# Filter generation at the start: the two table subtractions, the first weights' sums and two fetches change engine and place

## The chip, the cores and the metric

One NeuronCore of a Trainium2 chip runs the whole program. The metric is the device time of one execution in microseconds, lower is better; the median of a few executions stands for a kernel.

## What is computed

Four trunk layers follow each other over 512 latent and 256 context tokens of width 1024: latent attention, windowed attention, a gated long convolution, and latent attention again. Each has an adaLN modulation from `w_mod`. Only the long convolution's filters matter here. They depend on weights and positions alone, so the kernel makes them at its very start:

```python
z = jnp.concatenate([t, jnp.cos(bands * w), -jnp.sin(bands * w)], axis=-1)
h = jnp.sin(freq * (z @ f_w1 + f_b1))
h = jnp.sin(freq * (h @ f_w2 + f_b2))
h = (h @ f_w3).astype(jnp.float32).reshape(n, 2, C_ORDER, C_WIDTH)
return h * jnp.exp(-t[:, :, None, None] * deltas)
...
k = jnp.concatenate([lag0, h_fwd[1:], jnp.zeros((1, C_WIDTH)), h_bwd[:0:-1]], axis=0)
kf = jnp.fft.rfft(k, axis=0)
```

`n` is 512 for the latent and 256 for the context tokens, and both are done together as 768 columns.

## The kernel before

A Python program writes instructions in priority order; a planner then fixes the order of each engine at compile time, by a simulated timeline: an engine takes the earliest written instruction that is ready in that simulation. On the chip each engine works its list in that order, and waits at the head of it where an operand is late. All loads and stores are issued by SyncE, whose queue is in order too.

Exact fp32 products are made from pairs of a rounded "high" part and the "low" remainder: ScalarE copies a tile to fp32r (high), and VectorE or GpSimd subtracts it from the original (low). Then TensorE does three products (high·high, high·low, low·high).

Staging memory is one arena cut into slots of 1024 words; a slot's next user waits for its last reader.

The start, in the order written in `run`: `conditions` (L362), the first part of `filters` (up to the first `yield`, L1422), `setup` (L370: identity, modulation biases, `g_pre`), and then `M.pump` (L1681), which starts the first two `w_mod` fetches. After that a loop takes one step of the filters, and at given steps a unit of modulation or the first normalisation of a token tile (`pre`).

The first part of `filters`:

- the position network: step 0 is a matmul (L1329), a chain of six VectorE instructions that reduce the argument of the sine (L1333 to L1338), and the sine on ScalarE (L1339); step 1 is the same with the second weights (L1331). After step 1, L1344 and L1345 make the high and low parts of `h2`, the network's output;
- written between the two steps: `load_w3(0, 0)` fetches four blocks of `f_w3` (L1296), GpSimd makes their sum and difference (L1299, L1300), ScalarE and VectorE split it (L1302, L1303); and `load_ft(0)` fetches the first Fourier table (L1313: 128x1024 and 128x256), split by ScalarE (L1314) and GpSimd (L1315);
- after step 1: `load_ft(1)`, the second table, in the same way, and six loads of the decay (L1359).

Then eight groups (`taps`, `spectrum`) follow. `taps` of a group makes six tiles: two matmuls of `h2` with the split weights (L1380), the multiplication with the decay on VectorE (L1382; in two tiles of half the groups also the bias, L1384), the high part on ScalarE (L1386) and the low part on GpSimd for five tiles, on VectorE for one (L1388). Three buffers hold the products. `spectrum` multiplies these with a Fourier table (L1408), the first table for even groups, the second for odd ones, and VectorE and a store finish it (L1412 to L1418). `load_w3` comes again three times, at the odd groups, for the next weights.

The low parts of `h2` (L1345) must be there before the first L1380. The second and third decay tile lie in the memory that the network's tiles `zt`, `h` and `tm` leave.

Of the kernel before, what the change touches and what calls it, by code (L numbers as in the profile page):

```python
# [12 lines left out]
F32 = mybir.dt.float32  # L13
# [3 lines left out]
ALU = mybir.AluOpType  # L17
# [118 lines left out]
class Ring:  # L136
# [6 lines left out]
    def next(self):  # L143
        self.i += 1
        return self.blocks[self.i % len(self.blocks)]
# [125 lines left out]
class Kern:  # L271
# [989 lines left out]
    def filters(self, j):  # L1261

        nc, io = self.nc, self.io
# [15 lines left out]
        h2 = self.rl(T)  # L1279
        ft = self.rl(2 * 2 * 1280)  # L1280
        ftv = ft.v(2, 2, 1280)
# [6 lines left out]

        def load_w3(c, o):

            st = self.fs(1024)
            sv = st.v(2, 512)
            for d in range(2):
                c0 = d * 2048 + o * 1024 + 512 * c
                for half in range(2):
                    nc.sync.dma_start(out=sv[64 * half:64 * half + 64, d], in_=w3[:, c0:c0 + 512])  # L1296
            sd = self.fs(1024)
            sdv = sd.v(2, 512)
            nc.gpsimd.tensor_tensor(sdv[:, 0], sv[:, 0], sv[:, 1], op=ALU.add)  # L1299
            nc.gpsimd.tensor_tensor(sdv[:, 1], sv[:, 0], sv[:, 1], op=ALU.subtract)  # L1300
            wv = w3r.next().v(2, 2, 512)
            nc.scalar.activation(wv[:, 0], sdv, AF.Copy)  # L1302
            nc.vector.tensor_tensor(wv[:, 1], sdv, wv[:, 0].bitcast(F32), op=ALU.subtract)  # L1303
            st.free()
            sd.free()
            wvs[c, o] = wv
            biases[c, o] = bias = biasr.next()
            nc.sync.dma_start(out=bias.ap[0:1], in_=io["c_filt_bias"][j, o:o + 1, 512 * c:512 * c + 512])

        def load_ft(i):  # L1310
            for c0, n in ((0, 1024), (1024, 256)):
                st = self.fs(n)
                nc.sync.dma_start(out=st.ap, in_=io["ftab"][:, i, c0:c0 + n])  # L1313
                nc.scalar.activation(ftv[:, i, 0, c0:c0 + n], st.ap, AF.Copy)  # L1314
                nc.gpsimd.tensor_tensor(ftv[:, i, 1, c0:c0 + n], st.ap, ftv[:, i, 0, c0:c0 + n].bitcast(F32), op=ALU.subtract)  # L1315
                st.free()

        two_pi = 2 * math.pi
# [5 lines left out]
        for step in range(2):  # L1324
            for c0, n in CH:
                ps = self.a()[:, 0:n]
                for i, r in enumerate((lower, upper)):
                    if step == 0:
                        nc.tensor.matmul(ps[r], w1, zt.ap[:, TH * i + c0:TH * i + c0 + n], start=True, stop=True, skip_group_check=True)  # L1329
                    else:  # L1330
                        nc.tensor.matmul(ps[r], w2[r], h.ap[r, c0:c0 + n], start=True, stop=True, skip_group_check=True)  # L1331
                hv, tv = h.ap[:, c0:c0 + n], tm.ap[:, c0:c0 + n]
                nc.vector.tensor_scalar(hv, ps, fv[:, 2 * step:2 * step + 1], freq, op0=ALU.add, op1=ALU.mult)  # L1333
                nc.vector.tensor_scalar(tv, hv, 1.0 / two_pi, magic, op0=ALU.mult, op1=ALU.add)
                nc.vector.tensor_scalar(tv, tv, magic, None, op0=ALU.subtract)
                nc.vector.scalar_tensor_tensor(hv, tv, -c1, hv, op0=ALU.mult, op1=ALU.add)
                nc.vector.scalar_tensor_tensor(hv, tv, -c2, hv, op0=ALU.mult, op1=ALU.add)
                nc.vector.tensor_scalar(hv, hv, 3.1415925, -3.1415925, op0=ALU.min, op1=ALU.max)  # L1338
                nc.scalar.activation(hv, hv, AF.Sin)  # L1339
                if step == 1:  # L1340

                    for i, (r, o) in enumerate(((lower, upper), (upper, lower))):
                        c = slice(TH * i + c0, TH * i + c0 + n)
                        nc.scalar.activation(h2.ap[r, c], hv[r], AF.Copy)  # L1344
                        nc.vector.tensor_tensor(h2.ap[o, c], hv[r], h2.ap[r, c].bitcast(F32), op=ALU.subtract)  # L1345
            if step == 0:
                load_w3(0, 0)
                load_ft(0)
        for b in (zt, h, tm):
            b.free()  # L1350
        load_ft(1)
        LTS = [4, 5, 0, 1, 2, 3]
        decr = [self.fl(512) for _ in range(8)]
        tmps = Ring(self, "fl", 512, 3)
# [12 lines left out]
        def taps(c, o, e):  # L1367
# [3 lines left out]
            if e == 1 and (c, o) != (1, 1):  # L1371
                load_w3(*((c, 1) if o == 0 else (1, 0)))
                if (c, o) == (0, 1):
                    load_dec(1, 0)
                    load_dec(1, 1)
# [285 lines left out]
    def run(self, layers=(0, 1, 2, 3)):  # L1661
        nc, io = self.nc, self.io
        n = len(layers)
        self.layers = layers
        self.xd = {layers[0]: [io["xc"][P * t:P * t + P] for t in range(6)]}
        for i, L in enumerate(layers):
            if i < n - 1:
                d = self.dram.tile([T, D], F32, name=f"x{L + 1}")
                self.xd[L + 1] = [d[P * t:P * t + P] for t in range(6)]
            else:  # L1670
                self.xd[L + 1] = [io["out"][P * t:P * t + P] for t in range(io["out"].shape[0] // P)]
        L = layers[0]
        self.plan_mod(layers)
        self.set_swing("R")
        h = self.h_alloc()
        self.conditions()
        steps = self.filters(0) if 2 in layers else iter(())
        next(steps, None)
        self.setup()
        self.M.cap_d = self.M.look_d = 2  # L1680
        self.M.pump()  # L1681
        for i, L in enumerate(layers):
            kind, j = L % 3, L // 3
            ctx_out = L < DEPTH - 1
            if kind == 0:
                self.want_A(L, j, ctx_out)
            elif kind == 1:
                self.want_B(L, j)
            else:
                self.want_C(L, j)  # L1690
        L = layers[0]

        def pres():
            ts = [0, 1, 2, 3, 4, 5]
            self.W.cap_d = 2
            xts = [self.load_x(L, t) for t in ts[:1]]
            yield
            for i, t in enumerate(ts):
                if i < 5:
                    xts.append(self.load_x(L, ts[i + 1]))  # L1700
                self.pre(L, t, xts[i], h)
                xts[i].free()
                if i == WP:
                    self.turns_f = 1
                    self.W.pump()
                    self.turns_f = 6
                yield

        start = iter(pres())
        for i in range(99):  # L1710
            if i == LS:
                self.setup_late()
            if i == MI[3] - 1:
                self.M.cap_d = self.M.look_d = 0
            if i in MI:
                for _ in self.mod_ab_unit(L, MI.index(i)):
                    pass
            if i >= PS and (i - PS) % PD == 0:
                next(start, None)
            if i in WX:  # L1720
                self.W.cap_d, self.W.cap_w = WX[i]
                self.W.pump(*WX[i])
            if next(steps, 1) == 1 and i > PS + 13:
                break
        self.M.cap_d = self.M.look_d = 1
        for i, L in enumerate(layers):
            kind, j = L % 3, L // 3
            last = i == n - 1
            ctx_out = L < DEPTH - 1
            if kind == 0:  # L1730
                h = self.layer_A(L, j, h, ctx_out, last)
            elif kind == 1:
                h = self.layer_B(L, j, h, last)
            else:
                h = self.layer_C(L, j, h, last)
# [103 lines left out]
```

## Time and profile before

| | us |
|---|---|
| median of 3 runs | 1951.43 (1951.01 to 1953.01) |
| the profiled execution | 1952.31 |
| its span | 1950.4 |

The profile is one execution: its span starts with the first instruction of an engine, and some 1.9 us of the time lie around it. A row of the timeline says when an instruction began, how long it (or the run of equal ones, "x4") took, on which engine and line, what it wrote and read, and in brackets how long the engine had been idle and what released it. Engines are PE (TensorE), PEld (its weight loads), DVE (VectorE), ACT (ScalarE), POOL (GpSimd); SPq is SyncE's queue of transfers.

### The profile page before, as it was taken

Reading aid. Unit: us, or ns where it says so; the run is one execution under the profiler, and the core shown is the slowest. Engines: PE = TensorE matmul, PEld = TensorE weight load, DVE = VectorE, ACT = ScalarE, POOL = GpSimd, SP = SyncE. Lnnn points to the kernel's source line nnn. Section 1 sums busy time; section 2 is a strip of 40 time slices with the busy share of each in tenths; the row PEclk is TensorE's granted clock in tenths of the full one; section 3 lists DMA queues with packets and bytes.
Section 4 is the critical chain, followed back from the end, with each engine's and each line's share of the span. In section 5 each row is a group of like instructions: output and inputs, shape, how many; then the busy total and the mean of one; then the engine's idle time right before and its main releaser. Section 6 shows DMA issues by size and latency. Waiting matters only on the chain. (4 is left out here: it accounts for less than half of the span.)

```text
span 1950.4 us, 30304 instructions
## 1 busy us (share of the span) xinstructions
PE 1818.6 (93%) x11628; PEld 1576.9 (81%) x11628; DVE 1169.7 (60%) x2365; ACT 814.3 (42%) x1688; POOL 519.7 (27%) x523
## 2 busy tenths in 40 slices
PE   5879799999999899999989999999989899999998
PEld 3657588999988888888868789999988677889986
DVE  6694134777755277777665456655566553477663
ACT  3473132555544255665654522222222352354451
POOL 5561000000213321222231444444434221000120
PEclk9899999999999999999999999999999899999999
DMA  7867431010133122222363622222222334310121
GB/s 219 261 172 230 150 80 30 23 33 34 55 108 109 55 65 67 77 77 66 107 207 108 200 81 77 76 76 71 72 64 71 107 127 140 97 33 23 44 66 65
DMA packets 186356, 186.31 MB, mean 96 GB/s; under 512 B 16600, under 2 KB 164952, under 8 KB 186212
## 3 DMA queue, kind: packets, MB, share of 16 engines
q1 hardware_dynamic: 186212, 184.39, 30.6%
q8 instruction: 91, 1.49, 0.3%
q14 instruction: 53, 0.43, 0.1%
HBM read 160.24 MB, written 24.12 MB: 95 GB/s over the span
## 5 line engine op out<-in xcount | busy, mean ns | idle before, releaser
L588 PE MATMUL pb<-arena_r 128*128 128x512 f32 (+1 forms) x1488 | 280.9, 342 | 1.9 <-DVE arena_f L567 1.0
L341 ACT ACTIVATE arena_r<-pa 128x384 fp32r<-128x384 f32 (+2 forms) x382 | 175.5, 479 | 206.1 <-PE pa L909 67.9
L588 PEld LDWEIGHTS pb<-arena_r 128*128 128x128 f32 x1488 | 230.1, 190 | 32.9 <-ACT arena_r L1462 1.5
L342 DVE TENSOR_TENSOR arena_r<-pa,arena_r 128x384 fp32r<-128x384 f32 (+2 forms) x382 | 199.5, 536 | 81.7 <-ACT arena_r L341 79.8
L588 PE MATMUL pa<-arena_r,swing_R 128*128 128x512 f32 (+1 forms) x816 | 165.9, 355 | 0.6 <-DVE arena_r L342 0.4
L588 PEld LDWEIGHTS pa<-arena_r,swing_R 128*128 128x128 f32 x816 | 132.2, 188 | 21.8 <-DVE arena_r L342 0.6
L884 PE MATMUL pb<-arena_r 128*128 128x384 f32 (+1 forms) x720 | 141.5, 337 | 3.0 <-ACT arena_r L341 1.8
L606 PE MATMUL pb<-arena_r 128*128 128x512 f32 x552 | 133.7, 394 | 1.6 <-ACT arena_r L230 1.3
L233 POOL TENSOR_TENSOR swing_R<-arena_f,swing_R 128x1024 fp32r<-128x1024 f32 (+1 forms) x33 | 76.2, 2313 | 192.0 <-ACT swing_R L230 142.5
L884 PEld LDWEIGHTS pb<-arena_r 128*128 128x128 f32 x720 | 119.1, 188 | 5.1 <-ACT arena_r L341 2.5
L606 PEld LDWEIGHTS pb<-arena_r 128*128 128x128 f32 x552 | 102.5, 188 | 25.1 <-ACT arena_r L230 1.8
L679 POOL TENSOR_TENSOR arena_f<-arena_f 128x128 f32<-128x128 f32 (+1 forms) x44 | 20.9, 475 | 362.8 <-DVE small L892 178.6
L233 POOL TENSOR_TENSOR arena_r<-swing_F,arena_r 128x1024 fp32r<-128x1024 f32 x36 | 88.0, 2448 | 88.7 <-ACT arena_r L230 83.5
L358 POOL TENSOR_SCALAR small<-small 128x1 f32<-128x1 f32 x68 | 17.8, 261 | 348.0 <-ACT trash L564 139.5
L923 PE MATMUL pa<-arena_r 128*128 128x256 f32 x624 | 91.5, 286 | 2.1 <-DVE arena_r L342 2.1
L923 PEld LDWEIGHTS pa<-arena_r 128*128 128x128 f32 x624 | 81.9, 189 | 4.8 <-ACT arena_r L341 2.5
L1079 PE MATMUL pa<-swing_R,arena_r 128*128 128x256 f32 x576 | 80.3, 289 | 5.0 <-DVE arena_f L348 3.8
L230 ACT ACTIVATE arena_r<-swing_F 128x1024 fp32r<-128x1024 f32 x39 | 41.4, 1063 | 103.9 <-PE pb L588 63.3
L888 DVE TENSOR_REDUCE small<-pb 128x1 f32<-128x768 f32 (+1 forms) x80 | 67.5, 845 | 21.6 <-PE pb L884 20.7
L891 ACT ACTIVATE arena_f<-pb,small 128x768 f32<-128x768 f32 (+1 forms) x80 | 65.2, 817 | 33.1 <-DVE small L889 26.7
L1079 PEld LDWEIGHTS pa<-swing_R,arena_r 128*128 128x128 f32 x576 | 72.9, 192 | 7.3 <-DVE arena_f L348 5.2
L442 PE MATMUL pa<-arena_f,cst 128*32 128x256 f32 x744 | 56.7, 405 | 21.7 <-DMA arena_f<-in_w_mod_dram 21.6
(268 smaller groups left out, 4210.0 us busy)
## 6 DMA issues: line engine op xcount, KB each, us to landing
arena_f<-in_w_mod_dram SPq DMA_DIRECT2D x93, 512.0 KB, 4.7
swing_F<-in_c_w_in_dram SPq DMA_DIRECT2D x31, 512.0 KB, 5.0
kd<-arena_f SPq DMA_DIRECT2D x48, 256.0 KB, 3.5
arena_f<-in_a_w_in_dram SPq DMA_DIRECT2D x24, 512.0 KB, 3.7
arena_f<-kd SPq DMA_DIRECT2D x16, 768.0 KB, 5.2
arena_f<-in_b_w_in_dram SPq DMA_DIRECT2D x20, 512.0 KB, 3.7
x<-arena_f SPq DMA_DIRECT2D x18, 512.0 KB, 4.2
arena_f<-in_a_w_out_dram SPq DMA_DIRECT2D x16, 512.0 KB
```

The costliest lines, as they stand in the source:

```text
L230: nc.scalar.activation(hi, view, AF.Copy)
L233: eng.tensor_tensor(lo, view, hi.bitcast(F32), op=ALU.subtract)
L341: self.nc.scalar.activation(hi, src, AF.Copy)
L342: self.nc.vector.tensor_tensor(lo, src, hi.bitcast(F32), op=ALU.subtract)
L442: nc.tensor.matmul(ps[32 * j:32 * j + 32, n0:n0 + 256], self.cst[:, 4 * kh + j, :], w[:, j, :], start=(kh == 0), stop=(kh == 1), skip_grou ...
L588: nc.tensor.matmul(out, l, rhs(part, k, i), start=(k == 0 and q == 0), stop=(k == kt - 1 and q == 2))
L606: nc.tensor.matmul(ys[:, 512 * hf:512 * hf + 512], ov[:, a, k - ks.start], wt[:, 0, 512 * hf:512 * hf + 512], start=(k == 0 and q == 0), s ...
L884: nc.tensor.matmul(S[:, 512 * b:512 * b + w], l, r[:, k0 + w * b:k0 + w * b + w], start=(q == 0), stop=(q == 4))
L888: nc.vector.tensor_reduce(mx, Sv, axis=AX.XY, op=ALU.max)
L891: nc.scalar.activation(pr.v(nb, w), Sv, AF.Exp, bias=mx, scale=sc, accum_out=sm)
L923: nc.tensor.matmul(o[:, 0:256], vv[:, a_, kt % 3, P * hh:P * hh + P], ptv[i // nh][:, b_, i % nh], start=(i == 0 and q == 0), stop=(i == n ...
L1079: nc.tensor.matmul(ps[:, 0:256], self.h_at(h, part, k, P * t, P), w, start=(k == 0 and i == 0), stop=(k == KD - 1 and i == 2))
```

## The change

The first weights' sum and difference move from GpSimd to VectorE, and their split is written after step 1 instead of before it. The first table is still fetched between the steps, but its split is written after step 1, with the subtraction on VectorE. The second table's fetch gets a one-column VectorE copy from `h2` into its staging slot, so that the transfer can't start before the first high part of `h2` is there; its subtraction stays on GpSimd. The later three `load_w3` are as before. `M.pump` comes before `setup`.

```diff
         def load_w3(c, o):
 
+            split_w3(c, o, sum_w3(nc.gpsimd, fetch_w3(c, o)))
+
+        def fetch_w3(c, o):
             st = self.fs(1024)
             sv = st.v(2, 512)
             for d in range(2):
                 c0 = d * 2048 + o * 1024 + 512 * c
                 for half in range(2):
                     nc.sync.dma_start(out=sv[64 * half:64 * half + 64, d], in_=w3[:, c0:c0 + 512])
+            return st
+
+        def sum_w3(eng, st):
+            sv = st.v(2, 512)
             sd = self.fs(1024)
             sdv = sd.v(2, 512)
-            nc.gpsimd.tensor_tensor(sdv[:, 0], sv[:, 0], sv[:, 1], op=ALU.add)
-            nc.gpsimd.tensor_tensor(sdv[:, 1], sv[:, 0], sv[:, 1], op=ALU.subtract)
+            eng.tensor_tensor(sdv[:, 0], sv[:, 0], sv[:, 1], op=ALU.add)
+            eng.tensor_tensor(sdv[:, 1], sv[:, 0], sv[:, 1], op=ALU.subtract)
+            st.free()
+            return sd
+
+        def split_w3(c, o, sd):
+            sdv = sd.v(2, 512)
             wv = w3r.next().v(2, 2, 512)
             nc.scalar.activation(wv[:, 0], sdv, AF.Copy)
             nc.vector.tensor_tensor(wv[:, 1], sdv, wv[:, 0].bitcast(F32), op=ALU.subtract)
-            st.free()
             sd.free()
...
-        def load_ft(i):
+        def fetch_ft(i, late):
+            out = []
             for c0, n in ((0, 1024), (1024, 256)):
                 st = self.fs(n)
+                if late:
+
+                    nc.vector.tensor_copy(st.ap[0:64, 0:1], h2.ap[0:64, 0:1].bitcast(F32))
                 nc.sync.dma_start(out=st.ap, in_=io["ftab"][:, i, c0:c0 + n])
+                out.append((i, c0, n, st))
+            return out
+
+        def split_ft(eng, parts):
+            for i, c0, n, st in parts:
                 nc.scalar.activation(ftv[:, i, 0, c0:c0 + n], st.ap, AF.Copy)
-                nc.gpsimd.tensor_tensor(ftv[:, i, 1, c0:c0 + n], st.ap, ftv[:, i, 0, c0:c0 + n].bitcast(F32), op=ALU.subtract)
+                eng.tensor_tensor(ftv[:, i, 1, c0:c0 + n], st.ap, ftv[:, i, 0, c0:c0 + n].bitcast(F32), op=ALU.subtract)
                 st.free()
...
             if step == 0:
-                load_w3(0, 0)
-                load_ft(0)
+                sd0 = sum_w3(nc.vector, fetch_w3(0, 0))
+                ft0 = fetch_ft(0, False)
+        split_w3(0, 0, sd0)
+        split_ft(nc.vector, ft0)
         for b in (zt, h, tm):
             b.free()
-        load_ft(1)
+        split_ft(nc.gpsimd, fetch_ft(1, True))
...
         next(steps, None)
-        self.setup()
         self.M.cap_d = self.M.look_d = 2
         self.M.pump()
+        self.setup()
```

## Rows read from the trace of the kernel before

**Rows 1.** Stretches: length, busy time per engine (instructions), TensorE's clock, DMA share, GB/s.
```profile
10.00:20.00 10.00, 1.38 (x4) 0.13 (x4) 8.37 (x6) 3.67 (x5) 9.72 (x6) 1.00 1.07 368
20.00:60.00 40.00, 34.12 (x180) 23.64 (x181) 30.28 (x49) 18.58 (x32) 24.43 (x19) 1.00 0.69 211
...
240.00:1950.00 1710.00, 1632.33 (x10574) 1444.43 (x10573) 1031.11 (x2130) 715.61 (x1503) 420.12 (x419) 0.99 0.26 80
```

**Rows 2.** Timeline of VectorE, 5 to 26 us: both network steps, first tap.
```profile
6.19 0.68 DVE L1333 TENSOR_SCALAR arena_f<-pa,arena_f 128x384 f32<-128x384 f32 x1 [4.37 <-PE pa L1329]
...
7.29 0.36 DVE L1335 TENSOR_SCALAR arena_f<-arena_f 128x384 f32<-128x384 f32 x1
...
8.87 0.36 DVE L1338 TENSOR_SCALAR arena_f<-arena_f 128x384 f32<-128x384 f32 x1
11.53 0.68 DVE L1333 TENSOR_SCALAR arena_f<-pa,arena_f 128x384 f32<-128x384 f32 x1 [2.30 <-PE pa L1331]
...
13.02 2.40 DVE L1335 TENSOR_SCALAR arena_f<-arena_f 128x384 f32<-128x384 f32 x1
...
16.34 3.35 DVE L1303 TENSOR_TENSOR arena_r<-arena_f,arena_r 128x1024 fp32r<-128x1024 f32 x1
...
20.72 0.36 DVE L1338 TENSOR_SCALAR arena_f<-arena_f 128x384 f32<-128x384 f32 x1
22.29 1.14 DVE L1345 TENSOR_TENSOR arena_r<-arena_f,arena_r 64x384 fp32r<-64x384 f32 x2 [1.20 <-ACT arena_r L1344]
25.86 0.69 DVE L1382 TENSOR_TENSOR arena_f<-pa,arena_f 128x512 f32<-128x512 f32 x1 [2.43 <-PE pa L1380]
```

**Rows 3.** Timeline of GpSimd, 8 to 62 us; then stretches of GpSimd alone (busy, clock, DMA share, GB/s).
```profile
10.28 1.26 POOL L1299 TENSOR_TENSOR arena_f<-arena_f 128x512 f32<-128x512 f32 x1 [8.73 <-DMA arena_f<-in_c_f_w_dram]
...
12.72 7.55 POOL L1315 TENSOR_TENSOR arena_r<-arena_f,arena_r 128x1024 fp32r<-128x1024 f32 x4
28.01 2.52 POOL L1388 TENSOR_TENSOR swing_R<-arena_f,swing_R 128x512 fp32r<-128x512 f32 x2 [7.73 <-ACT swing_R L1386]
...
31.72 2.35 POOL L1300 TENSOR_TENSOR arena_f<-arena_f 128x512 f32<-128x512 f32 x1
...
28.00:45.00 17.00, 16.00 (x11) 1.00 0.69 222
45.00:145.00 100.00, 60.80 (x48) 0.95 0.74 216
```

**Rows 4.** Timeline of VectorE after 30 us; two short stretches, columns as in rows 1.
```profile
30.64 1.69 DVE L1384 SCALAR_TENSOR_TENSOR arena_f<-arena_f 1x512 f32<-1x512 f32 x1
32.25 0.67 DVE L1388 TENSOR_TENSOR swing_R<-arena_f,swing_R 128x512 fp32r<-128x512 f32 x1
...
35.86 1.78 DVE L1303 TENSOR_TENSOR arena_r<-arena_f,arena_r 128x1024 fp32r<-128x1024 f32 x1
...
69.84 1.22 DVE L1303 TENSOR_TENSOR arena_r<-arena_f,arena_r 128x1024 fp32r<-128x1024 f32 x1
...
34.00:36.00 2.00, 1.84 (x24) 0.99 (x16) 2.00 (x5) 1.74 (x3) 2.00 (x3) 1.00 0.09 20
...
69.80:71.10 1.30, 1.14 (x17) 0.56 (x18) 1.30 (x3) 1.04 (x2) 0.71 (x2) 1.00 1.07 321
```

**Rows 5.** Timeline of ScalarE, 11 to 13 us.
```profile
11.56 1.06 ACT L1314 ACTIVATE arena_r<-arena_f 128x1024 fp32r<-128x1024 f32 x1 [1.77 <-DMA arena_f<-in_ftab_dram]
```

**Rows 6.** Timeline of SyncE's queue, 0 to 60 us.
```profile
9.55 1.82 SPq L1359 DMA_DIRECT2D arena_f<-in_decay_dram x4
...
13.59 0.93 SPq L211 DMA_DIRECT2D arena_f<-in_w_mod_dram x2
...
23.49 0.81 SPq L1359 DMA_DIRECT2D arena_f<-in_decay_dram x2
```

**Rows 7.** Transfers issued from 7.6 to 40 us: count, KB each, median us to landing.
```profile
arena_f<-in_decay_dram SPq DMA_DIRECT2D x8, 256.0 KB, 5.8
arena_f<-in_ftab_dram SPq DMA_DIRECT2D x2, 512.0 KB, 5.0
```

## Prediction, made before the changed kernel had been run

> **What bounds the kernel now.** I read the stretches first [rows 1]. From 240 us to the end TensorE is busy 1632.3 of 1710 us, so that part is TensorE's own work, and time saved or lost before it moves it as a block. At the start it is otherwise: between 10 and 20 us TensorE has four matmuls (1.4 us), while GpSimd is busy 9.7 of 10 us, VectorE 8.4, and the DMA engines all the time; from 20 to 60 us TensorE is at 34 of 40 us and the DMA share falls to 0.69. The question is therefore what keeps TensorE from its first tap, and how much of a gain there lives until 240 us.
>
> The timeline of VectorE answers the first half [rows 2]. The first tap needs both parts of h2, and the network's second step makes them. Its six instructions take 3.04 us in step 0 (6.19 to 8.87 + 0.36) and 9.55 us in step 1 (11.53 to 20.72 + 0.36), the same six with L1303 among them. L1335 takes 2.40 us there against 0.36 in step 0; L1303 takes 3.35. All this lies beside GpSimd's four table subtractions, 12.72 to 20.27 [rows 3]. h2 is complete at 22.29 + 1.14 = 23.43.
>
> Is it GpSimd or the full DMA engines that slow VectorE? L1303 tells them apart [rows 4]: 1.78 us at 35.86, with GpSimd busy throughout and a DMA share of 0.09; 1.22 us at 69.84, with a DMA share of 1.07 and GpSimd busy for 0.71 of 1.30 us. So it is GpSimd, and the premise of the change holds.
>
> The Trainium skill (SBUF — State Buffer, Who interferes with whom) has it as a lock: a VectorE instruction with two SBUF inputs, or in a two-port mode, excludes a GpSimd instruction that reads SBUF, and the second to start is blocked fully. The rows of step 1 agree (L1335 waits 2 us, it isn't shared out). The same rule speaks against the change's other end: the second table's subtraction, still on GpSimd, would lie beside L1384, which has two SBUF inputs. It took 1.69 us at 30.64 beside L1300's 2.35, against the 0.67 of VectorE's other 512-column subtraction at 32.25 [rows 4], so by the rule the sum would be 1.0 us worse; without it nothing is lost there.
>
> **The change part by part.**
>
> *Sums on VectorE.* They leave GpSimd (1.26 us each) and cost VectorE what a 128x512 subtraction costs, 0.67 [rows 3, 4]. The weights land by 10.28, so they run from there to 11.62, in the hole before L1333 (11.53): 0.1 us on the path. If that hole were gone they would cost 1.34.
>
> *Step 1 with GpSimd quiet.* From 11.62 the six take step 0's 3.04, to 14.7. Sine, high part and low part follow: from the end of L1338 (21.08) to 23.43 is 2.35 us [rows 2]. That gives h2 at 17.05.
>
> *Three subtractions that VectorE now has beside it.* L1303 (1.22) and the first table (1280 columns, by L1303's rate 1.5) are 2.7 us. They are written behind step 1, but the planner puts ready work into holes. The idle of 1.20 us before L1345 [rows 2] takes one of them. If the rest stands behind L1345, h2 stays at 17.05; if all stand before it, h2 comes at 17.05 + 1.5 = 18.55. I take the middle, 17.8, since nothing in the trace decides it: 5.6 us earlier than 23.43 (bounds 4.9 and 6.4).
>
> *Second table fetched late.* It leaves GpSimd's stretch before the taps and comes back inside them. Its 640 KB start after the first high part of h2, about 16 us, and land about 5 us later by the first table's 5.0 [rows 7], at 21 to 22. ScalarE's copy costs 1.06 [rows 5], so GpSimd gets it at 22 to 23, just when the first L1388 comes due (28.01 − 5.6 = 22.4). What it costs GpSimd has two bounds: by L1299's rate 1280/512 x 1.26 = 3.2 us, by half of 7.55 us 3.8 [rows 3]. From 28 to 45 us GpSimd is busy 16.0 of 17 us, so it has no room for 3.2 to 3.8 there. But in that stretch are the next weights' sums (1.29 and 2.35), which no tap needs until the third group, and after 45 us GpSimd is busy only 61 of 100 us. Where the table stands in the place of these sums and pushes them back, the price is near zero; where it stands ahead of the taps' low parts as well, 3.8. Only the odd groups' spectrum reads the table, and by the order written it comes behind the first taps of the third group. I take 1.4, nearer to zero, because the third group and the slack after 45 us can absorb it.
>
> *The two tiny copies* on VectorE: one column each; bounds are zero and 0.36, what 384 columns take in step 0. They fall into VectorE's 2.43 us hole before the first tap [rows 2]; behind them wait only the transfers. I take zero, 0.7 if the hole is gone.
>
> *Queue of transfers.* Ahead of the taps the queue has 640 KB less, which at 368 GB/s [rows 1] is 1.7 us; the first four decays (issued from 9.55) come earlier, which nobody waits for. Two decays wait for h2's last reader (23.49) [rows 6]. They now start about 5.6 us earlier, but into a queue that is still full, beside the late table. Each 256 KB is 0.7 us at that rate; the second tap needs one of them, behind the first tap, which itself came 2.43 us after h2 [rows 2]. Bounds: zero (the queue has drained) and 1.7 (the table ahead of them); I take zero, since what stands ahead of them was issued 4 us and more before (13.59 and earlier), and keep 1.7 for the range.
>
> *w_mod ahead of setup.* The two fetches at 13.59 go a little earlier, and bmod, gpre and the identity's place in the list later. The first user of w_mod and of bmod is the modulation unit that `run` calls four steps into the filters, which is after h2 in either kernel; nothing waits, zero. Were they to pass the decays they would cost their 1 MB, 2.8 us.
>
> **Sum:** 5.6 − 1.4 = 4.2 us. The profiled execution, 1952.3, becomes 1948.1; against the median, 1951.43 − 4.2 = 1947.2. After 240 us there is nothing to absorb it; between 60 and 240 us the waits for w_mod follow from earlier events and not from a fixed moment, so I let them move along.
>
> **Rivals.** Less than about 0.2% (3.9 us) can't be told from no change.
>
> *A, forecast:* 1945.5 to 1949, chance 0.40, of which 0.24 lies beyond 3.9 us.
>
> *B, the second table takes the place of the first:* GpSimd pays 3.8 us within the taps and the late decays another 0 to 1.7. That leaves 0 to 2 us, about 1950.2. For it: 16 of 17 us busy. Against it: the sums can give way. 0.25.
>
> *C, slower:* engines work in order, and the planner knows only simulated landings. If it puts the second table's copy and subtraction ahead of the first L1386 and L1388, GpSimd stands until the table has landed, then needs 1.06 + 3.2 before the first low part. Before, that came at 28.01. So a landing at 23.7 uses up the whole gain, and each us later costs one; at 28 the time is 1955.7. For it: DMA engines at 1.07. Against it: that landing would be 12 us after the issue, twice the 5.8 seen. A late table read by a spectrum that was planned early acts in the same way. 0.15.
>
> *D, it doesn't do what it says:* VectorE stays slow although GpSimd is quiet, because of the DMA engines. Then the chain keeps its 9.5 us, VectorE has 1.5 us more, and the time is 1953. L1303's two rows speak against it. 0.05.
>
> *E, more:* h2 at 17.05, no price on GpSimd: 6.4 us, 1945. It needs every subtraction in a hole. 0.15.
>
> **How the numbers follow.** Faster by over 0.2%: 0.24 of A, 0.15 of E, 0.03 of B, together 0.42. Within: 0.16 of A, 0.22 of B, 0.04 of D, 0.42. Slower: 0.15 of C and 0.01 of D, 0.16. The likeliest case is A, 1947.2. The range takes in A, B, D, E and the near part of C, where the table lands up to 2.5 us past the point of 23.7: 1943 to 1954. By itself A has 1945.5 to 1949.
>
> **What would show it.** Right: step 1's L1335 at 0.36 us; L1303 at 1.2; h2 complete at 17 to 18.6 us instead of 23.43; the first L1388 at 22 to 23; no GpSimd wait for the table's transfer; TensorE's last waits before 240 us some 4 us earlier. B shows as GpSimd's L1388 of the second group no earlier than before; C as an idle time on GpSimd or ScalarE released by in_ftab; D as L1335 still above 1 us. The forecast is wrong, too, if the planner, starting from other moments, orders the units of modulation or the stores of the filters in another way; the trace of before can't price that, and the range covers it only in part.

## The result: slower by 0.7%, and the profile after

| | before | after |
|---|---|---|
| median, us (4 executions each) | 1951.22 (1946.31 to 1953.01) | 1962.24 (1960.28 to 1964.89) |
| profiled execution | 1952.31 | 1963.88 |
| its span | 1950.4 | 1961.8 |

The ratio of after to before is 1.0071 [1.0057, 1.0086] (95% interval in brackets, here and below). The forecast was 4.2 us faster; it came 11 us slower, and outside the range (1943 to 1954).

Line numbers after the change: L1306, L1307 the weights' sums; L1314, L1315 their split; L1327 the one-column copies, L1328 the fetch of a table, L1334, L1335 its split; L1353 to L1359 chain and sine; L1364, L1365 the parts of `h2`; L1381 the decay; L1402 the tap's matmuls, L1404 times decay, L1406 bias, L1408 high part, L1410 low part; L1430 to L1440 the spectrum.

The timeline of VectorE, which answers [rows 2]:

```profile
10.46 0.69 DVE L1306 TENSOR_TENSOR arena_f<-arena_f 128x512 f32<-128x512 f32 x1 [1.07 <-DMA arena_f<-in_c_f_w_dram]
...
11.68 0.68 DVE L1353 TENSOR_SCALAR arena_f<-pa,arena_f 128x384 f32<-128x384 f32 x1
12.87 1.22 DVE L1315 TENSOR_TENSOR arena_r<-arena_f,arena_r 128x1024 fp32r<-128x1024 f32 x1 [0.51 <-ACT arena_r L1314]
14.01 0.35 DVE L1354 TENSOR_SCALAR arena_f<-arena_f 128x384 f32<-128x384 f32 x1
14.28 1.55 DVE L1335 TENSOR_TENSOR arena_r<-arena_f,arena_r 128x1024 fp32r<-128x1024 f32 x2
15.75 0.35 DVE L1355 TENSOR_SCALAR arena_f<-arena_f 128x384 f32<-128x384 f32 x1
...
19.47 0.21 DVE L1327 COPY arena_f<-arena_r 64x1 f32<-64x1 f32 x2
19.71 0.55 DVE L1365 TENSOR_TENSOR arena_r<-arena_f,arena_r 64x384 fp32r<-64x384 f32 x1
22.70 0.56 DVE L401 CAST maskb<-arena_f 128x768 bf16<-128x768 f32 x1 [2.44 <-DMA arena_f<-in_mask_dram]
23.18 0.68 DVE L1404 TENSOR_TENSOR arena_f<-pa,arena_f 128x512 f32<-128x512 f32 x1
23.89 0.68 DVE L1406 SCALAR_TENSOR_TENSOR arena_f<-arena_f 1x512 f32<-1x512 f32 x1
28.15 1.42 DVE L1404 TENSOR_TENSOR arena_f<-pa,arena_f 128x512 f32<-128x512 f32 x2 [3.58 <-DMA arena_f<-in_decay_dram]
29.60 1.23 DVE L1406 SCALAR_TENSOR_TENSOR arena_f<-arena_f 1x512 f32<-1x512 f32 x1
```

What the change was built for happened: the six instructions of step 1 take 0.35 to 0.68 us each again, and `h2` is complete at 19.71 + 0.55 = 20.26 instead of 23.43. Then three transfers are late. VectorE stands 2.44 us for the mask, which the plan has put ahead of the first tap, and 3.58 us for a decay tile ahead of the second. The mask costs the first tap less than its wait: VectorE begins with the third of TensorE's products, and TensorE has it at 22.42 (the sixth of the eight matmuls in the first line below), so the tap at 23.18 comes 0.8 us late. ScalarE and GpSimd stand for the second table; the timelines (TensorE 18 to 33 us, ScalarE 18 to 32, GpSimd 5 to 36, where before's was [rows 3]):

```profile
19.50 3.78 PE L1402 MATMUL pa<-arena_r 128*128 128x512 f32 x8 [7.96 <-DVE arena_r L1365]
...
26.78 1.36 ACT L1334 ACTIVATE arena_r<-arena_f 128x1024 fp32r<-128x1024 f32 x2 [7.38 <-DMA arena_f<-in_ftab_dram]
28.05 0.61 ACT L1408 ACTIVATE swing_R<-arena_f 128x512 fp32r<-128x512 f32 x1
...
27.92 3.51 POOL L1335 TENSOR_TENSOR arena_r<-arena_f,arena_r 128x1024 fp32r<-128x1024 f32 x2 [26.37 <-ACT arena_r L1334]
31.39 1.27 POOL L1410 TENSOR_TENSOR swing_R<-arena_f,swing_R 128x512 fp32r<-128x512 f32 x1
```

ScalarE was free from 19.40, and the first product lay ready at 24.57 (L1406), but its work list has the table's copy ahead of the first high part. The first tap is still early, 23.18 instead of 25.86, but the first low part on GpSimd starts at 31.39, where before had 28.01. SyncE's queue shows where the transfers stood, and answers [rows 6] (start, time to issue, line, what, how many):

```profile
18.59 0.38 SPq L400 DMA_DIRECT2D arena_f<-in_mask_dram  x1
19.07 1.75 SPq L1299 DMA_DIRECT2D arena_f<-in_c_f_w_dram  x3
20.91 1.01 SPq L1328 DMA_DIRECT2D arena_f<-in_ftab_dram  x2
22.02 0.84 SPq L1381 DMA_DIRECT2D arena_f<-in_decay_dram  x2
```

The table is issued at 20.91, behind the mask and three blocks of the next weights, and the two decays behind the table. The DMA engines are full from 24 us on, while the table and the decays land. Stretches of after (length; busy time and instructions of PE, PEld, DVE, ACT, POOL; TensorE's clock; DMA share; GB/s); those from 10, 20 and 240 us answer to [rows 1]:

```profile
24.00:26.00 2.00, 1.14 (x2) 0.42 (x2) 0.57 (x1) 0.00 (x0) 0.00 (x0) 1.00 1.00 362
26.00:28.00 2.00, 0.00 (x0) 0.00 (x0) 0.00 (x0) 1.22 (x2) 0.08 (x1) 1.00 1.01 319
...
10.00:20.00 10.00, 2.04 (x5) 0.78 (x6) 7.66 (x15) 3.87 (x6) 0.00 (x0) 1.00 0.94 308
20.00:60.00 40.00, 33.30 (x144) 20.76 (x143) 24.13 (x35) 13.73 (x22) 22.44 (x16) 1.00 0.65 194
88.40:161.40 73.00, 59.65 (x277) 42.16 (x278) 55.40 (x91) 42.97 (x80) 40.73 (x35) 0.88 0.66 190
240.00:1961.00 1721.00, 1641.74 (x10652) 1449.89 (x10650) 1035.57 (x2132) 717.41 (x1509) 420.06 (x422) 0.99 0.26 79
```

GpSimd is quiet from 10 to 20 us (0.00 against 9.72 us), and from 240 us on TensorE is busy 95% of the time, as before. In between the loss grows. The table of moments (us from the start; "spectrum" is L1434, L1412 before; "layer" the first normalised tile of the second, third and fourth layer) shows where:

| profiled kernel | `h2` | first low part | first spectrum | 12th | 24th, last | layer 2 | layer 3 | layer 4 | end |
|---|---|---|---|---|---|---|---|---|---|
| before | 23.4 | 28.0 | 32.9 | 83.1 | 149.8 | 559.8 | 1031.4 | 1540.9 | 1950.4 |
| after | 20.3 | 31.4 | 38.7 | 88.4 | 161.4 | 574.4 | 1043.3 | 1552.5 | 1961.8 |

In these two profiles 5.8 us are lost by the first spectrum, another 6.3 us between the 12th and the last and 3.0 in the first layer, and later layers give 3 back. A profile is one execution. Two kernels of the experiments, e11 and e4, run TensorE's list in before's order, and so are two more samples of it: their spans are 1943.7 and 1941.9, the first spectrum comes at 33.4 and 33.7, and the 12th to the last take 65.5 and 65.2 us. The losses of 5.8 and 6.3 us stand clear of that spread; what the later layers give back does not, since layers 2 to 4 took 1590.6 us in before but 1584.9 and 1583.3 in e11 and e4, and 1587.4 in after. The stretch from the 12th to the last spectrum in the kernel before:

```profile
83.10:149.80 66.70, 51.20 (x242) 36.71 (x241) 54.65 (x90) 41.03 (x77) 38.88 (x33) 0.92 0.67 189
```

After does 35 more matmuls in it (e11 and e4, in before's order, 5 and 6 more), so its order is another one, and at a mean clock of 0.88 instead of 0.92.

### The profile page after: what moved, and what is told of

It reads as the page before. It is cut to its first block, busy times and chain, and to the rows that moved or that the text cites. A ratio compares the mean times of both kernels' runs of the same rounds, so it can differ in the third digit from the quotient of the medians.

```text
span 1961.8 us, 30305 instructions
## 1 busy us (share of the span) xinstructions
PE 1829.0 (93%) x11628; PEld 1578.9 (80%) x11628; DVE 1172.5 (60%) x2371; ACT 814.2 (42%) x1688; POOL 508.4 (26%) x519
## 5 line engine op out<-in xcount | busy, mean ns | idle before, releaser
L588 PE MATMUL pa<-arena_r,swing_R 128*128 128x512 f32 (+1 forms) x816 | 165.9, 355 | 0.6 <-DVE arena_r L342 0.4
L606 PE MATMUL pb<-arena_r 128*128 128x512 f32 x552 | 133.7, 394 | 2.1 <-ACT arena_r L230 1.8
L606 PEld LDWEIGHTS pb<-arena_r 128*128 128x128 f32 x552 | 102.5, 188 | 25.4 <-ACT arena_r L230 2.0
L891 ACT ACTIVATE arena_f<-pb,small 128x768 f32<-128x768 f32 (+1 forms) x80 | 65.2, 816 | 33.1 <-DVE small L889 26.7
L1060 PE MATMUL pa<-arena_r,swing_R 128*128 128x512 f32 (+1 forms) x384 | 74.2, 342 | 2.7 <-DVE arena_r L1086 1.1
```

Source lines behind the costliest of these rows:

```text
L588: nc.tensor.matmul(out, l, rhs(part, k, i), start=(k == 0 and q == 0), stop=(k == kt - 1 and q == 2))
L606: nc.tensor.matmul(ys[:, 512 * hf:512 * hf + 512], ov[:, a, k - ks.start], wt[:, 0, 512 * hf:512 * hf + 512], start=(k == 0 and q == 0), s ...
L891: nc.scalar.activation(pr.v(nb, w), Sv, AF.Exp, bias=mx, scale=sc, accum_out=sm)
L1060: nc.tensor.matmul(o, l[:, k], self.h_at(h, part, k, t0, n), start=(k == 0 and i == 0), stop=(k == KD - 1 and i == 2))
```

## The experiments

Two theories. **Late transfers**: the loss is the waits for decay, mask and table at the first taps; remove these and the change gains 0 to 4 us. **Another plan**: the planner starts from other simulated moments and gives the whole program another order, good or bad by some us, whatever happens at the start. All ratios are to the kernel before, run beside on the same chip; its median was 1948.55, 1946.83 and 1947.67 us in the three sets of runs (20, 28 and 25 executions), each on another chip. The traces also give the order in which TensorE ran its 11628 matmuls. The last column counts the places of that list at which a kernel has another matmul than before has (by the text of its source line, its tiles and its shape); after has 541.

| kernel | median, us | ratio | first low part | first spectrum | last | end of profiled span | places |
|---|---|---|---|---|---|---|---|
| e1 table not held | 1955.51 | 1.0035 [1.0020, 1.0050] | 27.4 | 35.3 | 152.1 | 1953.8 | 493 |
| e2 table behind taps | 1960.08 | 1.0056 [1.0032, 1.0080] | 28.5 | 33.6 | 153.0 | 1954.1 | 585 |
| e3 decays moved | 1947.32 | 1.0002 [0.9985, 1.0018] | 22.7 | 39.9 | 151.5 | 1944.0 | 441 |
| e5 both of these | 1978.30 | 1.0166 [1.0123, 1.0210] | 22.7 | 35.3 | 156.6 | 1980.7 | 2010 |
| e14 e3, mask later | 1979.59 | 1.0171 [1.0151, 1.0191] | 25.1 | 35.2 | 152.0 | 1979.9 | 1832 |
| e9 VectorE part only | 1959.64 | 1.0060 [1.0042, 1.0078] | 27.6 | 36.0 | 154.1 | 1950.7 | 493 |
| e13 e9, decays moved | 1952.59 | 1.0025 [1.0012, 1.0039] | 25.5 | 31.7 | 151.3 | 1947.6 | 802 |
| e6 e1, decays moved | 1953.55 | 1.0029 [1.0013, 1.0045] | 25.5 | 31.7 | 152.3 | 1944.8 | 802 |
| e8 hold only | 1949.00 | 1.0012 [0.9997, 1.0027] | 25.8 | 33.3 | 156.1 | 1944.9 | 506 |
| e7 before, decays moved | 1952.70 | 1.0029 [1.0012, 1.0047] | 26.0 | 32.7 | 153.7 | 1943.1 | 580 |
| e11 before, one column | 1948.82 | 1.0007 [0.9994, 1.0020] | 27.7 | 33.4 | 148.6 | 1943.7 | 0 |
| e4 w_mod early only | 1946.74 | 1.0003 [0.9988, 1.0018] | 27.9 | 33.7 | 148.5 | 1941.9 | 0 |

**Is it the late table?** e1 fetches it early again, e2 holds it still longer, behind the first two taps, with the split behind the first group.

```diff
 # e1
-        split_ft(nc.gpsimd, fetch_ft(1, True))
+        split_ft(nc.gpsimd, fetch_ft(1, False))
 # e2, against after
-                    nc.vector.tensor_copy(st.ap[0:64, 0:1], h2.ap[0:64, 0:1].bitcast(F32))
+                    nc.vector.tensor_copy(st.ap[:, 0:1], sds[0, 0, 0][:, 5, 0, 0:1].bitcast(F32))
...
-        split_ft(nc.gpsimd, fetch_ft(1, True))
...
+                if g == (0, 0, 0) and n == 0:
+                    ft1 = fetch_ft(1, True)
                 yield
+            if g == (0, 0, 0):
+                split_ft(nc.gpsimd, ft1)
```

> The changed kernel, but the second table's fetch is not held back (no one-column copies from h2); the table's subtraction stays on GpSimd, written after step 1, and all else is as changed. Theory T (the late table costs it: its transfer goes out at 20.9 us, lands at 26.8, ScalarE and GpSimd stand behind it, and two decays stand behind it in the queue of transfers): ScalarE's 7.4 us wait for in_ftab is gone, the first low part on GpSimd comes at 25 to 28 us instead of 31.4, and the time is 1947 to 1953. Rival P (the planner, started from other moments, orders all later work worse, whatever the table does): the time stays at 1957 or above. Rival V (the subtractions that VectorE took into the network's chain are the cost): h2 at 20 us or later and 1957 or above.

> The changed kernel, but the second table is fetched after the first two taps (its one-column copies read a tap's high part instead of h2) and its split is written behind the first group's taps. T: nothing of the table stands ahead of the first taps' high and low parts, so the first low part comes at 24 to 27 us, and the time is 1945 to 1952; the decays that wait for h2 may still land late, as three blocks of the next weights stand ahead of them. P: 1957 or above. If the decays alone set it (rival D2): the second tap's wait for in_decay stays at 3 us or more and the time is 1952 to 1957.

Half of the loss is gone in e1, and its time lies between the two ranges expected: nothing waits for the table, but `h2` is back at 22.45. The first table on VectorE meets the second one on GpSimd:

```profile
14.04 3.70 DVE L1335 TENSOR_TENSOR arena_r<-arena_f,arena_r 128x1024 fp32r<-128x1024 f32 x2
17.66 0.88 DVE L1355 TENSOR_SCALAR arena_f<-arena_f 128x384 f32<-128x384 f32 x1
...
15.17 2.56 DVE L1335 TENSOR_TENSOR arena_r<-arena_f,arena_r 128x256 fp32r<-128x256 f32 x1
...
15.02 3.29 POOL L1335 TENSOR_TENSOR arena_r<-arena_f,arena_r 128x1024 fp32r<-128x1024 f32 x2 [13.47 <-ACT arena_r L1334]
```

3.70 us where after has 1.55: without the hold the quiet GpSimd isn't had. The 3.70 are two instructions ("x2"). The one of 1024 columns, which began before GpSimd's, took its usual 1.2; the one of 256, which began after it, took 2.56 (third line), where after's took 0.42. In e2 the table is out of the way and the first low part comes 2.9 us earlier than in after, yet the mask (3.27 us) and the decay (1.76 us) still stop VectorE, and another 7.1 us are lost between the last spectrum and the second layer; the time is in the range of the second theory. So the late table explains a part, and what follows it is not simply its shadow.

**Is it the decay behind the table?** The two late decays are the tiles that take over the network's memory. e3 turns the ring of eight blocks by three, so that they lie in memory that nobody uses at that time; e5 does that to e2.

```diff
-            b, lt = decr[(6 * c + n) % 8], LTS[n]
+            b, lt = decr[(6 * c + n + 3) % 8], LTS[n]
...
-                        decr[(6 + 6 + n) % 8].free()
+                        decr[(6 + 6 + n + 3) % 8].free()
```

> The changed kernel, but the decays use their eight blocks from the fourth one on, so that none of the first six has to wait for the memory of the network's tiles; they are all issued early. T: the second tap's 3.6 us wait for in_decay is gone, but ScalarE still waits for the table until 26 us or later, so the first low part stays at 30 us or later and the time falls by no more than 3 us, 1959 to 1963. D2 (the decays set it): 1952 to 1957. P: any time, without relation to these waits.

> Both edits of the two runs before: the second table behind the first taps, and the decays in blocks that nobody else uses. T together with the decays: VectorE waits for no transfer between h2 and the sixth tap, the first low part comes at 23 to 26 us, two to five us before that of the kernel before (28.0), and the time is 1944 to 1949. P: 1957 or above.

e3 is the largest gain among the variants, and only the second theory, which named no time, allows it: all six decays are issued by 11.9 us, none is waited for, the first low part starts at 22.7 and the end is that of the kernel before. Its start is not good, though: the mask (2.79 us), the sinks (3.43 us) and the next weights take the place of the decay, and the first spectrum comes at 39.9, later than in any other. What it gains it gains after that: from the 12th to the last spectrum it takes 60.8 us, before 66.7 and after 73.0, in an order that is neither's (738 places of TensorE's list differ from after's, all but 191 of them ahead of the second layer). So it shows that after's loss can be had back with these two tiles moved, not that their wait alone was the loss. It shows, too, that a first spectrum 7.0 us late need not cost anything at the end.

e5 should have had the best of both and is 1.7% slower, some 30 us. Of these 23 are not at the start. They lie between the second and the third layer, the windowed attention. That stretch in before and in e5 (stretches, columns as above):

```profile
559.80:1031.40 471.60, 443.69 (x3220) 384.90 (x3219) 302.90 (x713) 243.39 (x591) 123.20 (x152) 0.99 0.29 93
...
565.60:1060.30 494.70, 453.48 (x3237) 389.23 (x3236) 305.76 (x714) 244.48 (x593) 123.06 (x152) 0.98 0.28 89
```

TensorE has 17 matmuls more there, is busy 9.8 us longer and stands 41 us instead of 28: no filter, table or decay is touched there. The order is: between these two moments all kernels of the table but e5 and e14, and after too, have before's order of TensorE at every place, and take 466 to 472 us; e5 differs from it at 1071 of 3218 places. That is the second theory, in its plainest form.

**What does another order cost by itself?** e11 changes nothing but one column of zeros written on VectorE; e7 turns the decays in the kernel before; e4 has only `M.pump` ahead of `setup`.

```diff
 # e11
                 load_w3(0, 0)
                 load_ft(0)
+                nc.vector.memset(fv[:, 140:141], 0.0)
 # e4
-        self.setup()
         self.M.cap_d = self.M.look_d = 2
         self.M.pump()
+        self.setup()
```

> The kernel before with one VectorE instruction more, a memset of one column that nobody reads, 0.1 us, behind step 0's chain; everything else is written as before. The planner nevertheless orders most of the program in another way. T: the time stays within 2 us of the kernel before, as no wait is added. P: it moves by 3 us or more, and the move arises after the first taps.

> The kernel before with the decays in their blocks from the fourth one on, as in the run on the changed kernel that gained 13 us by it. T: the second tap of the kernel before doesn't wait for its decay, so there is little to gain: 0 to 3 us under the kernel before. P: any move of 3 us or more, as the plan is another one.

> The kernel before with only w_mod's first fetches ahead of setup. The orders of TensorE, VectorE, ScalarE and GpSimd are those of the kernel before, so both theories give ratio 0.999 to 1.001. The rival price: if w_mod's 1 MB passes the decays or the mask in the queue, the first taps wait up to 2.8 us longer, ratio 1.0015.

The expectation of e11 says that the planner orders most of the program in another way. It did not: in the traces TensorE, ScalarE and GpSimd run before's list at every place, and VectorE's has the one instruction more. So e11 doesn't test another order; it and e4 repeat the kernel before, with no change of time that can be measured. e7 has another order: its first low part comes 2.0 us earlier, its first spectrum 0.2, and its end is 0.29% worse, as the second theory allows and the first does not. From the 12th to the last spectrum it takes as long as after, though no transfer is late in its start (the stretch in e7, columns as above):

```profile
80.80:153.70 72.90, 58.30 (x280) 42.35 (x280) 53.77 (x89) 42.17 (x77) 39.62 (x36) 0.91 0.68 202
```

e4 puts four transfers of SyncE's list in another place and changes no other engine's list, and no time: the early `w_mod` is neutral.

**The parts of the change.** e8 is the hold alone, on the kernel before; e9 the VectorE part alone, with the early table and `setup` first.

```diff
 # e8
                 st = self.fs(n)
+                if i == 1:
+                    nc.vector.tensor_copy(st.ap[0:64, 0:1], h2.ap[0:64, 0:1].bitcast(F32))
 # e9, against after
-        split_ft(nc.gpsimd, fetch_ft(1, True))
+        split_ft(nc.gpsimd, fetch_ft(1, False))
...
+        self.setup()
         self.M.cap_d = self.M.look_d = 2
         self.M.pump()
-        self.setup()
```

> The kernel before with one part of the change alone: the second table's fetch held back by the one-column copies from h2, all else as before. h2 comes at about 21 us, as GpSimd has one table less beside VectorE. T (the late table costs it): ScalarE waits for in_ftab, the first low part comes at 30 us or later instead of 28.0, and the end of the filters (the last of the 24 high parts of the spectrum, 149.8 us before) is 2 to 8 us later; the time is 2 to 8 us above the kernel before. P (the planner's later order sets it): the end of the filters or the later layers move by as much in either direction, without relation to that wait.

> The kernel before with the other part alone: the first sums and the first table's subtraction on VectorE, the second table fetched early and subtracted on GpSimd after step 1, w_mod behind setup as before. h2 at 20 to 22 us, first low part at 26 to 28. T: no loss, the time is 0 to 3 us under the kernel before. P: as in the run without the hold (0.35 per cent above), since the order of the engines is that of another plan: 4 to 10 us above.

The hold alone is the milder part. `h2` is at 21.1, because only half of GpSimd's subtractions lie beside step 1. VectorE waits 1.72 us for a decay, but ScalarE has the first high part ahead of the table's copy, which starts at 25.66 without a wait, and the 4.12 us on GpSimd stand behind the first low part. Its last spectrum is 6.3 us late, yet at the end no loss can be told from the noise (1.0012). The VectorE part alone costs 0.6%, more than either theory expected, although `h2` comes 0.8 us earlier than before. This ratio repeats only roughly: e1 has e9's order on the four engines and differs from it in the same four transfers as e4 from before, and came out at 1.0035 on another chip. The intervals of the two just meet.

**The VectorE part with nothing late.** e13 and e6 are e9 and e1 with the decays turned as in e3. They have the same order on TensorE, VectorE, ScalarE and GpSimd and differ in the place of four transfers in SyncE's list. e14 is e3 with `LS = 12` instead of 2, which writes the mask and the late constants ten steps later.

> VectorE part alone (sums and first table on VectorE, second table fetched early, setup first), with the decay tiles in blocks that the network does not use. Late-transfer theory: what the VectorE part alone loses, 0.6%, is again a wait for a transfer at the first taps, so it goes: ratio to the kernel before 0.999 to 1.001, the first low part on GpSimd at 26 to 27.5 us, the first spectrum by 33. Plan theory: the waits of the start are not it; the loss lies in another order of the whole program, and an edit of the start that changes moments only draws another one: ratio anywhere from 0.998 to 1.01, without regard to when the first spectrum comes.

> The changed kernel with the second table fetched early (no one-column copies) and the decay tiles moved. Late-transfer theory: neither table nor decay can be late; h2 at about 22.5 us, first low part at 26, first spectrum before 33, ratio to the kernel before 0.998 to 1.000. Plan theory: ratio anywhere from 0.998 to 1.01.

> The changed kernel with the decay tiles moved and with the mask and the small late constants (0.8 MB) written ten steps of the filters later. Late-transfer theory: VectorE's wait for the mask and a part of the waits for the next weights and the table go; first low part at 22.7 as with the decays moved alone, first spectrum at 33 to 36 instead of 39.9, ratio to the kernel before 0.997 to 0.999, the first version that is faster. Plan theory: first spectrum earlier, but the end not, ratio 1.000 or above.

e13 and e6 agree with each other, 1.0025 and 1.0029. Neither waits for a decay, mask or table, the first low part is 2.5 us and the first spectrum 1.2 us earlier than before: the start that the prediction wanted, if a smaller one. And both are some 5 us slower at the end than before, run beside them. In the profile of e13 the lead is gone by the 12th spectrum and 1.5 us are lost by the last. So a better start doesn't carry through this kernel by itself, and what undoes it lies behind 32 us. The first theory missed here (0.999 to 1.001 and 0.998 to 1.000); the range of the second, 0.998 to 1.01, holds both, but it is too wide to be much of a test.

e14 has a better start than e3 (first spectrum 35.2, VectorE without a wait for the mask), should have been the first version that is faster, and loses 22.8 us in the windowed attention, like e5. The two have the same order of TensorE there, place by place, and the same length; e3, which has before's order there, for comparison (e14, then e3):

```profile
565.60:1059.90 494.30, 453.76 (x3237) 389.87 (x3236) 306.07 (x713) 244.97 (x593) 122.73 (x152) 0.98 0.28 89
...
559.60:1029.00 469.40, 440.68 (x3219) 382.62 (x3218) 302.66 (x712) 243.07 (x591) 122.75 (x152) 0.99 0.29 94
```

At the end of that layer TensorE's timeline in e14 has a wait of 3.95 us for VectorE's L567, the addition of a finished output tile to its tokens, ahead of the last matmuls (L606):

```profile
1051.97 1.88 PE L494 MATMUL pa<-arena_f,sel 128*128 128x512 f32 x4
1057.80 7.16 PE L606 MATMUL pb<-swing_R,arena_r 128*128 128x512 f32 x18 [3.95 <-DVE arena_f L567]
```

The same wait, 3.95 us, stands in e5 at this layer's end, and in no other kernel. (At the end of the third layer every kernel has one like it, before at 1538.89 with 3.93 us.) That is 4 of the 23 us; the rest is spread over many short waits and the longer busy time. So the 23 us go with this one order of the layer, in both kernels that have it and in none of the others; which places of the order carry them, and why the planner chose it, stays open.

## Why the prediction was wrong

**The reading of the bottleneck was right.** GpSimd did slow step 1. With it quiet, the six instructions of the chain take 0.35 to 0.68 us, while the DMA share is 0.94. Rival D is out. e1 shows the reverse: with GpSimd back, 3.70 instead of 1.55 us, all of the difference in the instruction that began second. That agrees with the lock that the prediction quoted from the Trainium skill (SBUF — State Buffer, Who interferes with whom). The price that the prediction named for the lock's other end, 1.0 us, came out at about half: L1406 took 1.23 us at 29.60 beside GpSimd's table, against 0.68 at 23.89. One of the prediction's readings was weaker than it says. L1303 at 35.86 runs until 37.64, for the most part outside the stretch from 34 to 36 us whose DMA share of 0.09 it quotes; in its own 1.78 us the share was 0.88. So these rows didn't part GpSimd from the DMA engines as cleanly as claimed; the run of after did.

**Three subtractions in holes: half right.** I took 17.8 (17.05 to 18.55). All three stand inside the chain, L1315 between its first and second instruction and both L1335 between the second and third; L1315 waits 0.51 us for ScalarE besides. The chain runs from 11.68 to 17.69, 6.0 us, instead of 3.04 and at most 1.5 more, and `h2` is at 20.26. 2.5 us of the 5.6 were missing here. The step that failed: the bound for "if all stand before it", 18.55, still credited the 1.20 us hole before the low part to one of them; the planner put all three further ahead. The two tiny copies, taken at zero, stand between the two low parts and cost 0.2 us.

**The second table: sized by a quiet queue.** I had it issued at 16 us, landed at 21 to 22, ready for GpSimd at 22 to 23. It was issued at 20.91, because its copy follows `h2` and because the mask and three blocks of weights stood ahead in the queue, and was there at 26.78: 5.9 us after its issue. The landing time of [rows 7], 5.0, was nearly right; the moment of issue was not. The price on GpSimd, taken as 1.4, was 31.39 − 28.01 = 3.4 us against before, on top of the 3.2 us of lead in `h2`, so 6.5 us.

**The term "Queue of transfers", taken at zero, was the main failure at the start.** The upper bound was 1.7 us, for the table ahead of the decays. VectorE waited 3.58 us for the decay, and the mask, which the sum didn't have, held the first tap back by 0.8. The trace of before had the hint: those decays are issued only after the network's tiles have been read for the last time, by the low part of `h2` that ends at 23.43 [rows 2, 6]. With `h2` 3.2 us earlier they were issued only 1.5 us earlier (22.02 for 23.49), behind mask, weights and now the table, and the second tap began at 28.15. I took zero because what stood ahead of them had been issued 4 us and more before. In the changed kernel it was not only the 640 KB of the table that came ahead of precisely those two tiles, but the mask and the next weights too.

**Rival C was the case**: ScalarE and GpSimd, in order, stood until the second table had landed. I gave it 0.15 because a landing at 28 us "would be 12 us after the issue", which started from the issue at 16; and by that same issue a landing at 23.7, where C begins to cost, would have been under 8. By the working of C, a landing at 26.8 gives 1952.3 + 3.1 = 1955.4; the profiled execution took 1963.9. So C has the mechanism by which the first low part came 3.4 us later than before's, and not the size of the whole.

**Letting everything after the start "move along" was wrong, and so was "the range covers it only in part" as a footnote.** Of the 11.4 us between the two profiles, 5.8 are there at the first spectrum. The 6.3 from the 12th to the last come in another order of the same work; that this order costs them is likely but not shown for after itself. For it speak e7, which loses as much there with nothing late, and e3, which starts later than after and loses nothing there. Nor is it shown that the 5.8 us reach the end. e13 and e6 end 0.25 to 0.29% slower with a start in which nothing is late; e5 and e14 show that an order can cost 23 us in a layer far away; e3, that it can cost nothing. Of the eleven kernels with another order, after and ten variants, none was faster than before: nine came out at 1.0002 to 1.0071 and two at 1.017. A rigid shift of all that follows was the wrong model for a kernel whose order is planned as a whole: the change should have been priced with such a spread on top.

**Not settled**: how after's 11 us divide between its late transfers and its order, why the VectorE part costs 0.25% with nothing late at the start (a difference of the size by which e1 and e9 differ), and which places of the order carry the 23 us. One companion of the loss is shown, not its direction: the mean clock. In the 28 executions of before in the second set of runs, the time falls by 1.0 us for each 0.001 of mean granted clock (0.981 to 0.990, correlation −0.73). The means were 0.9855 for these, 0.9836 and 0.9841 for e13 and e6, 0.9819 for e9, 0.9815 for after. At that slope 4 of after's 11 us go with the clock, 1 to 2 of e13's and e6's 5. In after's profile 14 of the 20 stretches of 10 us with a lowered clock have TensorE busy for less than 9 us, of the 176 at the full clock 30. So waits and a lower clock go together; no run tells which brings which.

No variant beats the kernel before by more than can be measured; e3, e8, e11 and e4 can't be told from it.

## What to carry to other kernels

When a step is made faster, list what was issued on the strength of its end (here decays that take its memory, a table held back by its result) and ask when those land in the queue as it will then be: an earlier reader doesn't make an earlier transfer. A load that is held back must be placed by what stands beside it in the queue at that time and ahead of what it passes, and its first use checked in the order of each in-order engine. Where the order is planned as a whole, compare the engines' lists of the two kernels before a gain of 0.2% at the start is believed: where the order differs, the spread of orders was larger than the effect. Do the same with an edit that is meant as a control, for it may leave the order as it was.

## What the runs showed that I had not expected

- One more instruction on VectorE, a column of zeros, left every other engine's order as it was (e11, 1.0007 [0.9994, 1.0020]); two plans that differ by where the decay tiles lie differ by 1.1% (e5 against e2, 1.0166 to 1.0056).
- Of 1950 us, 23 hang on the order of one layer: 494 to 495 us in both kernels that have the one order, 466 to 472 in the twelve that have the other.
- Executions of one kernel spread by ±7 us (before: 1939.5 to 1953.4 in one set of runs), and about half of the variance goes with the granted clock; a profile's span is one draw of it. e9's profiled span was 1950.7, equal to before's, while its median was 0.6% longer.
- A VectorE subtraction of 1280 columns took 1.55 us with GpSimd idle (after) and 3.70 us beside GpSimd's subtraction of the same size, which itself took 3.35 (e9).
- VectorE's wait before the first tap [rows 2], which the trace gives to TensorE, is not TensorE's: with the decays in other memory it is 0.73 us (e7) while the matmuls start at the same moment (22.62 against 22.89). It came from the order in which the products were taken: e7's VectorE begins with TensorE's first product, before's with the third.
